# A row-wise log-sum-exp: the second pass as a section with its own semaphores, a shorter reduce in the check, and the first two loads issued as four transfers each, of every fourth partition

## The chip, the cores and the metric

The kernel runs on one core of one Trainium2 chip. The metric is the device time of that core in microseconds (us). All runs quoted here are at a granted clock of 1.000. A run's time is its profiled span plus 1.8 us, so differences in span can be compared with differences in time. Some words of this text: an *issue* is the instruction that starts a transfer; the DMA engines carry the transfer out in *packets*; it has *landed*, or is *complete*, with the last of its sixteen completions in the trace; an engine is *drained* when its own instructions are done and it goes to the final barrier.

## The reference

```python
batch, seq, dim = 32, 512, 1024
x = np.random.randn(batch, seq, dim).astype(np.float32)

max_x = np.max(x, axis=-1, keepdims=True)
return (max_x.squeeze(-1) + np.log(np.sum(np.exp(x - max_x), axis=-1))).astype(np.float32)
```

There are 16,384 rows of 1,024 values: 67.1 MB in, 64 KB out.

## The kernel before

Each of the 128 partitions holds 128 consecutive rows of `x`. The kernel skips the maximum: it takes `log(sum(exp(x)))` straight away, checks afterwards that no sum left a safe range, and only if one did does it run a second, stable pass. With this input it never does. The first two loads carry 16 rows per partition, which is one run of 64 KB in each partition.

```python
RING = 48
loads = [
    "R8 R8", "R8 R8", "R8 R8", "R7 R6 A A", "R6 R5 A A A", "R5 R4 A", "R5 R4", "R5 T3",
    "R3 A A A", "R3 A", "R2 T2", "R3", "R1 A", "T2", "T1", "A", "A",
]
ENGINES = [mybir.EngineType.SP, mybir.EngineType.Activation, mybir.EngineType.DVE]
...
def load(p0, c0, size):
    return nc.sync.dma_start(out=ring[:, p0 : p0 + size, :], in_=x_rows[:, c0 : c0 + size, :])
...
# per load: ScalarE exponentiates; VectorE adds up (R, T), or ScalarE does it itself (A)
...
nc.scalar.activation(out=res[:, EARLY:NC], in_=sumexp[:, EARLY:NC], func=AF.Ln)
nc.sync.dma_start(out=out_view, in_=res)

# the check: sums 0..126 within [1e-15, 1e15], the last row's maximum, the last sum
nc.vector.tensor_scalar(out=clamped[:, 0:LAST], in0=sumexp[:, 0:LAST], ...)
nc.vector.scalar_tensor_tensor(out=clamped[:, 0:LAST], ..., accum_out=bad[:, 0:1])
nc.tensor.matmul(count, lhsT=bad[:, 0:1], rhs=far, start=True, stop=False)
nc.vector.reduce_max(out=bad[:, 2:3], in_=last_row[:, 0, 0 : d // 4], axis=AX.X)
nc.vector.tensor_scalar(out=bad[:, 1:2], in0=bad[:, 2:3], ..., op0=ALU.is_lt)
nc.tensor.matmul(count, lhsT=bad[:, 1:2], rhs=far, start=False, stop=False)
nc.tensor.matmul(count, lhsT=sumexp[:, LAST:NC], rhs=ones, start=False, stop=True)
nc.vector.tensor_scalar(out=fine, in0=count, scalar1=HIGH, scalar2=None, op0=ALU.is_lt)
all_fine = nc.values_load(fine[0:1, 0:1], engines=ENGINES, ...)   # the flag, into registers
with tc.If(all_fine < 1, preferred_fallthrough_block=False):
    ...  # the second pass, with loads and store on SyncE: not taken with this input
```

`ENGINES` lists who reads the flag and branches: SyncE, ScalarE and VectorE. All five engines then meet at a final barrier (in the trace of before their last waits start at 163.99 to 164.04 us, and the span ends at 164.09).

Of the kernel before, what the change touches and what calls it, by code (L numbers as in the profile page):

```python
# [13 lines left out]
@with_exitstack  # L14
def kernel(
    ctx: ExitStack,
    tc: tile.TileContext,
    x: bass.AP,
    out: bass.AP,
):  # L20
    nc = tc.nc
    P = nc.NUM_PARTITIONS
    fp32 = mybir.dt.float32
    i32 = mybir.dt.int32
    AF = mybir.ActivationFunctionType
    AX = mybir.AxisListType
    ALU = mybir.AluOpType

    x_flat = x.flatten_outer_dims()
    n, d = x_flat.shape  # L30
    assert n % P == 0
    NC = n // P
    H = d // 2

    x_rows = x_flat.rearrange("(p c) d -> p c d", p=P)
    out_view = out.rearrange("a b -> (a b)").rearrange("(p c) -> p c", p=P)
# [8 lines that stand above are left out]
    ]  # L45
    loads = [[(op[0], int(op[1:] or 1)) for op in load.split()] for load in loads]
    assert sum(s for ops in loads for _, s in ops) == NC
    ENGINES = [mybir.EngineType.SP, mybir.EngineType.Activation, mybir.EngineType.DVE]
    EARLY = 104
    LAST = NC - 1  # L50

    big = ctx.enter_context(tc.tile_pool(name="big", bufs=1))
    stats = ctx.enter_context(tc.tile_pool(name="stats", bufs=1))
    psum = ctx.enter_context(tc.tile_pool(name="psum", bufs=1, space=bass.MemoryType.PSUM))

    ring = big.tile([P, RING, d], fp32, name="ring")
    sumexp = stats.tile([P, NC], fp32, name="sumexp")
    res = stats.tile([P, NC], fp32, name="res")
    clamped = stats.tile([P, NC], fp32, name="clamped")
    bad = stats.tile([P, 3], fp32, name="bad")  # L60
    fine = stats.tile([1, 1], i32, name="fine")
    far = stats.tile([P, 1], fp32, name="far")
    ones = stats.tile([P, 1], fp32, name="ones")
    last_exp = psum.tile([P, 1, d], fp32, name="last_exp")
    count = psum.tile([1, 1], fp32, name="count")

    nc.scalar.preload_act_table_set("natural_log_exp_and_others")  # L67
    nc.vector.memset(ones, 1.0)  # L68
    nc.vector.memset(far, 100 * HIGH)

    def load(p0, c0, size):
        return nc.sync.dma_start(out=ring[:, p0 : p0 + size, :], in_=x_rows[:, c0 : c0 + size, :])  # L72

    def without_wait(ins, group, reason):

        tc.declare_no_dep(ins.ins, group=group, reason=reason)

    c = 0
    p = 0
    for ops in loads:  # L80
        size = sum(s for _, s in ops)
        if p + size > RING:
            p = 0
        dma = load(p, c, size).ins
        for how, s in ops:
            v = ring[:, p : p + s, :]
            sums = sumexp[:, c : c + s]
            if how == "A":
                o = v if c < LAST else last_exp
                exp = nc.scalar.activation(out=o, in_=v, func=AF.Exp, accum_out=sums)  # L90
            else:
                exp = nc.scalar.activation(out=v, in_=v, func=AF.Exp)  # L92
            without_wait(exp, "loads", "the slot's earlier users came before this load")
            without_wait(exp, "exps", "the slot's earlier users came before this load")
            without_wait(exp, "sums", "the slot's earlier users came before this load")
            tc.add_to_no_dep_group("exps", exp.ins)
            added = []
            if how == "R":
                added = [nc.vector.reduce_sum(out=sums, in_=v, axis=AX.X)]  # L99
            elif how == "T":  # L100
                for r in range(s):
                    lo = ring[:, p + r, 0:H]
                    added.append(
                        nc.vector.scalar_tensor_tensor(  # L104
                            out=lo, in0=lo, scalar=1.0, in1=ring[:, p + r, H:d],
                            op0=ALU.mult, op1=ALU.add, accum_out=sums[:, r : r + 1],
                        )
                    )
            for add in added:
                tc.declare_no_dep(add.ins, dma, reason="ScalarE has waited for it")  # L110
                without_wait(add, "loads", "they came before this one")
            for add in added:
                tc.add_to_no_dep_group("sums", add.ins)
            c += s
            p += s
            last_row = v
        tc.add_to_no_dep_group("loads", dma)
        if c == EARLY + 14:
            nc.scalar.activation(out=res[:, 0:EARLY], in_=sumexp[:, 0:EARLY], func=AF.Ln)  # L119

    nc.scalar.activation(out=res[:, EARLY:NC], in_=sumexp[:, EARLY:NC], func=AF.Ln)  # L121
    nc.sync.dma_start(out=out_view, in_=res)




    nc.vector.tensor_scalar(  # L127
        out=clamped[:, 0:LAST], in0=sumexp[:, 0:LAST],
        scalar1=LOW, scalar2=HIGH, op0=ALU.max, op1=ALU.min,
    )  # L130
    nc.vector.scalar_tensor_tensor(  # L131
        out=clamped[:, 0:LAST], in0=clamped[:, 0:LAST], scalar=0.0, in1=sumexp[:, 0:LAST],
        op0=ALU.bypass, op1=ALU.not_equal, accum_out=bad[:, 0:1],
    )
    nc.tensor.matmul(count, lhsT=bad[:, 0:1], rhs=far, start=True, stop=False)  # L135
    nc.vector.reduce_max(out=bad[:, 2:3], in_=last_row[:, 0, 0 : d // 4], axis=AX.X)  # L136
    nc.vector.tensor_scalar(  # L137
        out=bad[:, 1:2], in0=bad[:, 2:3], scalar1=LOG_LOW, scalar2=None, op0=ALU.is_lt
    )
# [4 lines that stand above are left out]
    all_fine = nc.values_load(  # L144
        fine[0:1, 0:1], engines=ENGINES, min_val=0, max_val=1,
        skip_runtime_bounds_check_because="a truth value",
    )
    with tc.If(all_fine < 1, preferred_fallthrough_block=False):
        for c0 in range(0, NC, RING):
            s = min(RING, NC - c0)  # L150
            v = ring[:, 0:s, :]
            neg = clamped[:, c0 : c0 + s]
            load(0, c0, s)
            nc.vector.tensor_reduce(out=neg, in_=v, op=ALU.max, axis=AX.X, negate=True)
            nc.vector.tensor_add(out=v, in0=v, in1=neg[:, :, None].to_broadcast([P, s, d]))
            nc.scalar.activation(out=v, in_=v, func=AF.Exp)
            nc.vector.reduce_sum(out=sumexp[:, c0 : c0 + s], in_=v, axis=AX.X)
        nc.scalar.activation(out=res, in_=sumexp, func=AF.Ln)
        nc.vector.tensor_sub(out=res, in0=res, in1=clamped)
        nc.sync.dma_start(out=out_view, in_=res)  # L160


# [28 lines left out]
```

## Time and profile before

| | before |
|---|---|
| time | 165.29 us, median of 3 (165.22 to 165.62) |
| profiled span | 164.1 us, in a run of 165.87 us |
| DMA engines busy | 95.7% of the span |
| VectorE, ScalarE busy | 74%, 71% |
| first load packet starts (packet records of the trace) | 1.75 us |
| first load complete, by its sixteenth completion (trace) | 22.99 us |
| last load complete (trace) | 159.68 us |
| from there to the end of the span | 4.41 us |

The profiled run was slower than the median by 0.6 us.

These are lines of the page of the kernel before: its busy row, the DMA row in 40 slices, the DMA queue's line and the chain of waits.

```profile
PE 0.4 (0%) x6; PEld 0.2 (0%) x6; DVE 122.2 (74%) x44; ACT 116.8 (71%) x53; POOL 0.2 (0%) x4
...
DMA  7979998997997999899999989999999999999960
...
q1 hardware_dynamic: 2592, 67.18, 95.7%
...
DMA 64%; DVE 22%; ACT 11%; issue 1%; SPq 0%; PE 0%; DVEq 0%
```

The DMA engines are the bound: only the last two slices show them busy for less than 70%. The timeline of the kernel before, 0 to 24 us (start, length, engine, line, operation), shows the head: SyncE's first three load issues, merged in one line, and ScalarE's first work, which starts as the first load is complete.

```profile
0.73 1.33 SPq L72 DMA_DIRECT2D ring<-in_x_dram  x3
...
23.01 7.03 ACT L92 ACTIVATE ring<-ring 128x8192 f32<-128x8192 f32 x1 [21.00 <-DMA ring<-in_x_dram]
```

The windows view of the kernel before has the DMA share and GB/s as its last two columns. A packet's bytes and time are entered where it starts, so a share above 1 in a short window means that several packets began there. Loads begin between 1.7 and 2.0 us.

```profile
0.00:1.70 1.70, 0.00 (x0) 0.00 (x0) 0.09 (x2) 0.97 (x1) 0.20 (x4) 1.00 0.00 0
1.70:2.00 0.30, 0.00 (x0) 0.00 (x0) 0.00 (x0) 0.30 (x1) 0.00 (x0) 1.00 5.14 1748
```

The timeline of the kernel before from 160.3 us on shows the tail: two operations on 127 columns, the reduce, the compare, the output store's issue, and the flag.

```profile
160.19 0.23 DVE L127 TENSOR_SCALAR clamped<-sumexp 128x127 f32<-128x127 f32 x1
160.45 0.29 DVE L131 SCALAR_TENSOR_TENSOR clamped<-clamped,sumexp 128x127 f32<-128x127 f32 x1
...
160.66 0.41 DVE L136 TENSOR_REDUCE bad<-ring 128x1 f32<-128x256 f32 x1
...
161.11 0.15 DVE L137 TENSOR_SCALAR bad<-bad 128x1 f32<-128x1 f32 x1
161.15 0.35 SPq L122 DMA_DIRECT2D out_dram<-res  x1
...
161.60 0.14 DVE L143 TENSOR_SCALAR fine<-count 1x1 int32<-1x1 f32 x1 [0.33 <-PE count L141]
```

The view of the tile `fine` lists who reads the flag and for how long (minimum, median and maximum in ns).

```profile
L144 SPq TENSOR_LOAD <-fine x1: 462/462/462, 161.8 to 161.8; - x1
L144 ACTq TENSOR_LOAD <-fine x1: 469/469/469, 161.8 to 161.8; - x1
L144 DVEq TENSOR_LOAD <-fine x1: 543/543/543, 161.8 to 161.8; - x1
```

After the flag come instructions that the timeline leaves out (branches, semaphore waits). Their records say: VectorE was drained at 163.22 us, SyncE at 163.40, and the span ended 0.69 us after SyncE.

### The profile page before, as it was taken

Reading aid. Unit: us, or ns where it says so; the run is one execution under the profiler, and the core shown is the slowest. Engines: PE = TensorE matmul, PEld = TensorE weight load, DVE = VectorE, ACT = ScalarE, POOL = GpSimd, SP = SyncE. Lnnn points to the kernel's source line nnn. Section 1 sums busy time; section 2 is a strip of 40 time slices with the busy share of each in tenths; the row PEclk is TensorE's granted clock in tenths of the full one; section 3 lists DMA queues with packets and bytes.
Section 4 is the critical chain, followed back from the end, with each engine's and each line's share of the span. In section 5 each row is a group of like instructions: output and inputs, shape, how many; then the busy total and the mean of one; then the engine's idle time right before and its main releaser. Section 6 shows DMA issues by size and latency. Waiting matters only on the chain.

```text
span 164.1 us, 205 instructions
## 1 busy us (share of the span) xinstructions
PE 0.4 (0%) x6; PEld 0.2 (0%) x6; DVE 122.2 (74%) x44; ACT 116.8 (71%) x53; POOL 0.2 (0%) x4
## 2 busy tenths in 40 slices
PE   0000000000000000000000000000000000000001
PEld 0000000000000000000000000000000000000000
DVE  0000000699959999399999995999998999979893
ACT  3000039990699708995399929999969599999992
POOL 0000000000000000000000000000000000000000
DMA  7979998997997999899999989999999999999960
GB/s 256 511 335 431 511 399 367 511 463 304 511 431 335 511 450 404 374 464 479 433 447 419 433 365 449 419 432 440 417 439 415 433 425 419 415 421 423 409 248 20
DMA packets 2594, 67.19 MB, mean 409 GB/s; under 512 B 288, under 2 KB 416, under 8 KB 800
## 3 DMA queue, kind: packets, MB, share of 16 engines
q1 hardware_dynamic: 2592, 67.18, 95.7%
q14 instruction: 2, 0.02, 0.0%
HBM read 67.11 MB, written 0.07 MB: 409 GB/s over the span
## 4 chain that ended last, share of the span: by engine, by line
DMA 64%; DVE 22%; ACT 11%; issue 1%; SPq 0%; PE 0%; DVEq 0%
DMA ring<-in_x_dram 64%; DVE sumexp L99 20%; ACT ring L92 11%; DVE ring L104 1%; SPq L72 0%; DVE bad L136 0%; DVE clamped L127 0%; PE count L140 0%; DVE bad L137 0%; DVE clamped L131 0%; DVE fine L143 0%; PE count L141 0%; DVEq L127 0%
## 5 line engine op out<-in xcount | busy, mean ns | idle before, releaser
L99 DVE TENSOR_REDUCE sumexp<-ring 128x8 f32<-128x8192 f32 (+7 forms) x20 | 116.2, 5854 | 38.2 <-ACT ring L92 38.2
L92 ACT ACTIVATE ring<-ring 128x8192 f32<-128x8192 f32 (+7 forms) x24 | 101.7, 4283 | 43.6 <-DMA ring<-in_x_dram 43.6
L90 ACT ACTIVATE ring<-ring 128x1024 f32<-128x1024 f32 x12 | 12.5, 1039 | 0.0
L104 DVE SCALAR_TENSOR_TENSOR ring<-ring 128x512 f32<-128x512 f32 x8 | 5.1, 684 | 0.0
L90 ACT ACTIVATION_READ_ACCUMULATOR ring<-ring 128x1 f32 x12 | 2.2, 186 | 0.0
L67 ACT ACT_TABLE_LOAD x1 | 1.3, 1283 | 0.7 <-PEq L175 0.7
L90 ACT ACTIVATE last_exp<-ring 128x1024 f32<-128x1024 f32 x1 | 1.0, 1005 | 0.0
L68 DVE MEMSET ones<- 128x1 f32 x1 | 0.1, 59 | 0.8 <-PEq L175 0.8
L104 DVE DVE_READ_ACCUMULATOR ring<-ring 128x1 f32 x8 | 0.7, 82 | 0.0
L135 PE MATMUL count<-far,bad 128*1 128x1 f32 x2 | 0.2, 164 | 160.8 <-DVE clamped L131 160.8
L136 DVE TENSOR_REDUCE bad<-ring 128x1 f32<-128x256 f32 x1 | 0.4, 415 | 0.0
L143 DVE TENSOR_SCALAR fine<-count 1x1 int32<-1x1 f32 x1 | 0.1, 145 | 0.3 <-PE count L141 0.3
L131 DVE SCALAR_TENSOR_TENSOR clamped<-clamped,sumexp 128x127 f32<-128x127 f32 x1 | 0.3, 290 | 0.0
L127 DVE TENSOR_SCALAR clamped<-sumexp 128x127 f32<-128x127 f32 x1 | 0.2, 227 | 0.1
L135 PEld LDWEIGHTS count<-far,bad 128*1 128x1 f32 x2 | 0.1, 80 | 160.8 <-DVE clamped L131 160.8
L119 ACT ACTIVATE res<-sumexp 128x104 f32<-128x104 f32 x1 | 0.3, 273 | 0.0
L121 ACT ACTIVATE res<-sumexp 128x24 f32<-128x24 f32 x1 | 0.2, 222 | 0.0
L140 PE MATMUL count<-far,bad 128*1 128x1 f32 x2 | 0.2, 164 | 0.3 <-DVE bad L137 0.3
L141 PE MATMUL count<-ones,sumexp 128*1 128x1 f32 x2 | 0.2, 164 | 0.0
L90 ACT ACTIVATION_READ_ACCUMULATOR last_exp<-ring 128x1 f32 x1 | 0.2, 185 | 0.0
L137 DVE TENSOR_SCALAR bad<-bad 128x1 f32<-128x1 f32 x1 | 0.2, 154 | 0.0
L141 PEld LDWEIGHTS count<-ones,sumexp 128*1 128x1 f32 x2 | 0.1, 82 | 0.0
(7 smaller groups left out, 0.6 us busy)
## 6 DMA issues: line engine op xcount, KB each, us to landing
ring<-in_x_dram SPq DMA_DIRECT2D x1, 7680.0 KB, 33.1
ring<-in_x_dram SPq DMA_DIRECT2D x1, 7168.0 KB, 30.7
ring<-in_x_dram SPq DMA_DIRECT2D x1, 5120.0 KB, 31.4
ring<-in_x_dram SPq DMA_DIRECT2D x1, 4608.0 KB, 33.7
ring<-in_x_dram SPq DMA_DIRECT2D x1, 4096.0 KB, 29.4
ring<-in_x_dram SPq DMA_DIRECT2D x2, 2048.0 KB, 32.7
ring<-in_x_dram SPq DMA_DIRECT2D x1, 3072.0 KB, 36.3
ring<-in_x_dram SPq DMA_DIRECT2D x2, 1024.0 KB, 38.8
```

Of the source, the lines that this page charges most:

```text
L67: nc.scalar.preload_act_table_set("natural_log_exp_and_others")
L90: exp = nc.scalar.activation(out=o, in_=v, func=AF.Exp, accum_out=sums)
L92: exp = nc.scalar.activation(out=v, in_=v, func=AF.Exp)
L99: added = [nc.vector.reduce_sum(out=sums, in_=v, axis=AX.X)]
L104: nc.vector.scalar_tensor_tensor(out=lo, in0=lo, scalar=1.0, in1=ring[:, p + r, H:d], op0=ALU.mult, op1=ALU.add, accum_out=sums[:, r : r + 1],
L119: nc.scalar.activation(out=res[:, 0:EARLY], in_=sumexp[:, 0:EARLY], func=AF.Ln)
L121: nc.scalar.activation(out=res[:, EARLY:NC], in_=sumexp[:, EARLY:NC], func=AF.Ln)
L127: nc.vector.tensor_scalar(out=clamped[:, 0:LAST], in0=sumexp[:, 0:LAST], scalar1=LOW, scalar2=HIGH, op0=ALU.max, op1=ALU.min,)
L131: nc.vector.scalar_tensor_tensor(out=clamped[:, 0:LAST], in0=clamped[:, 0:LAST], scalar=0.0, in1=sumexp[:, 0:LAST], op0=ALU.bypass, op1=AL ...
L135: nc.tensor.matmul(count, lhsT=bad[:, 0:1], rhs=far, start=True, stop=False)
L136: nc.vector.reduce_max(out=bad[:, 2:3], in_=last_row[:, 0, 0 : d // 4], axis=AX.X)
L141: nc.tensor.matmul(count, lhsT=sumexp[:, LAST:NC], rhs=ones, start=False, stop=True)
```

## The change

The second pass becomes a section with two semaphores of its own, all its transfers issued from ScalarE, so SyncE no longer reads the flag. The reduce in the check goes over 64 columns instead of 256. And each of the first two loads is issued as four transfers, of every fourth partition, so that each hands the DMA engines a quarter of the rows at a time.

```diff
-    ENGINES = [mybir.EngineType.SP, mybir.EngineType.Activation, mybir.EngineType.DVE]
+    ENGINES = [mybir.EngineType.Activation, mybir.EngineType.DVE]
...
     def load(p0, c0, size):
-        return nc.sync.dma_start(out=ring[:, p0 : p0 + size, :], in_=x_rows[:, c0 : c0 + size, :])
+        step = 4 if c0 < 2 * 16 else 1
+        return [
+            nc.sync.dma_start(
+                out=ring[k::step, p0 : p0 + size, :], in_=x_rows[k::step, c0 : c0 + size, :]
+            ).ins
+            for k in range(step)
+        ]
...
-    nc.vector.reduce_max(out=bad[:, 2:3], in_=last_row[:, 0, 0 : d // 4], axis=AX.X)
+    nc.vector.reduce_max(out=bad[:, 2:3], in_=last_row[:, 0, 0 : d // 16], axis=AX.X)
...
     with tc.If(all_fine < 1, preferred_fallthrough_block=False):
-        for c0 in range(0, NC, RING):
-            ...
-            load(0, c0, s)
-            ...
+        with tc.tile_critical(sync_engine=mybir.EngineType.Activation):
+            with nc.semaphore("landed") as landed, nc.semaphore("ready") as ready:
+                for c0 in range(0, NC, RING):
+                    ...
+                    nc.scalar.dma_start(out=v, in_=x_rows[:, c0 : c0 + s, :]).then_inc(landed, 16)
+                    ...
```

More of the change, by code (lines that the diff above doesn't have):

```diff
@@ L83 @@
             p = 0
-        dma = load(p, c, size).ins
+        dmas = load(p, c, size)
         for how, s in ops:
@@ L109 @@
             for add in added:
-                tc.declare_no_dep(add.ins, dma, reason="ScalarE has waited for it")
+                for dma in dmas:
+                    tc.declare_no_dep(add.ins, dma, reason="ScalarE has waited for it")
                 without_wait(add, "loads", "they came before this one")
@@ L116 @@
             last_row = v
-        tc.add_to_no_dep_group("loads", dma)
+        for dma in dmas:
+            tc.add_to_no_dep_group("loads", dma)
         if c == EARLY + 14:
@@ L148 @@
     with tc.If(all_fine < 1, preferred_fallthrough_block=False):
-        for c0 in range(0, NC, RING):
-            s = min(RING, NC - c0)
-            v = ring[:, 0:s, :]
-            neg = clamped[:, c0 : c0 + s]
-            load(0, c0, s)
-            nc.vector.tensor_reduce(out=neg, in_=v, op=ALU.max, axis=AX.X, negate=True)
-            nc.vector.tensor_add(out=v, in0=v, in1=neg[:, :, None].to_broadcast([P, s, d]))
-            nc.scalar.activation(out=v, in_=v, func=AF.Exp)
-            nc.vector.reduce_sum(out=sumexp[:, c0 : c0 + s], in_=v, axis=AX.X)
@@ L158 @@
-        nc.scalar.activation(out=res, in_=sumexp, func=AF.Ln)
-        nc.vector.tensor_sub(out=res, in0=res, in1=clamped)
-        nc.sync.dma_start(out=out_view, in_=res)
+        with tc.tile_critical(sync_engine=mybir.EngineType.Activation):
+            with nc.semaphore("landed") as landed, nc.semaphore("ready") as ready:
+                rows = 0
+                steps = 0
+                for c0 in range(0, NC, RING):
+                    s = min(RING, NC - c0)
+                    v = ring[:, 0:s, :]
+                    neg = clamped[:, c0 : c0 + s]
+                    if c0:
+                        nc.scalar.wait_ge(ready, steps)
+                    nc.scalar.dma_start(out=v, in_=x_rows[:, c0 : c0 + s, :]).then_inc(landed, 16)
+                    rows += 16
+                    nc.vector.wait_ge(landed, rows)
+                    nc.vector.tensor_reduce(
+                        out=neg, in_=v, op=ALU.max, axis=AX.X, negate=True
+                    ).then_inc(ready, 1)
+                    nc.vector.wait_ge(ready, steps + 1)
+                    nc.vector.tensor_add(
+                        out=v, in0=v, in1=neg[:, :, None].to_broadcast([P, s, d])
+                    ).then_inc(ready, 1)
+                    nc.scalar.wait_ge(ready, steps + 2)
+                    nc.scalar.activation(out=v, in_=v, func=AF.Exp).then_inc(ready, 1)
+                    nc.vector.wait_ge(ready, steps + 3)
+                    nc.vector.reduce_sum(
+                        out=sumexp[:, c0 : c0 + s], in_=v, axis=AX.X
+                    ).then_inc(ready, 1)
+                    steps += 4
+                nc.scalar.wait_ge(ready, steps)
+                nc.scalar.activation(out=res, in_=sumexp, func=AF.Ln).then_inc(ready, 1)
+                nc.vector.wait_ge(ready, steps + 1)
+                nc.vector.tensor_sub(out=res, in0=res, in1=clamped).then_inc(ready, 1)
+                nc.scalar.wait_ge(ready, steps + 2)
+                nc.scalar.dma_start(out=out_view, in_=res).then_inc(landed, 16)
+                nc.scalar.wait_ge(landed, rows + 16)
```

## The prediction

> **What bounds the kernel now.** The loads. The page counts 67.1 MB over the 164.1 us span (409 GB/s), the 16 DMA engines busy 95.7%; VectorE 74%, ScalarE 71%. In the chain of waits, loads of `ring` hold 64%. The trace's packets show first load packets from 1.75 us and the last load landing at 159.7 us; in between no DMA engine lacks work: each later load is issued about 30 us before it lands. A 64 KB packet takes 2.42 us, 27 GB/s; sixteen of those are 433 GB/s. The change moves the same bytes, so it can gain only at the ends: the head, and a tail of 4.4 us from the last landing to the span's end.
>
> **Head.** Today one issue queues 128 rows, eight 64 KB rows per DMA engine. The sixteen first packets start staggered, from 1.75 to 2.83 us, and the first load's completions spread from 22.20 to 22.99 us: an engine that starts late stays late. A first issue of 32 rows is two rows per engine; if the stagger is the time to hand out descriptors, it should shrink to about a quarter, 0.3 us. [...] Eight issues at 0.43 us (trace) take SyncE 3.4 us, but two rows per engine last 4.9 us, so nothing starves. The ninth transfer waits for the first quarter, about 7 us, with 14 MB still queued. Expected: first load complete 0.5 to 0.8 us sooner, last load 0.2 to 0.6 us. Later stages move along.
>
> **Tail.** SyncE today: output store issued 161.15, flag read 161.77 (0.46 us), branch, four semaphore updates, branch at 162.70, seven waits, drained at 163.40. VectorE drained at 163.23, ScalarE at 162.97; the store landed at 162.70. Without the flag read SyncE drains by about 162.9. VectorE then ends the kernel: 0.17 us gained. The reduce over 64 instead of 256 columns (0.415 us now, about 1 ns per column) takes 0.2 us from the chain reduce, compare, matmul, flag, read, branch; ScalarE's `sumexp`, ready at 160.87, does not take over. One more semaphore wait before that reduce should hide. Sum: 0.3 to 0.4 us.
>
> **Not on the path.** The second pass's section is not executed with this input; its waits stand inside the branch not taken. The final barrier remains.
>
> **Time.** 165.29 - 0.4 - 0.35, rounded up: 164.6 us, range 163.9 to 165.6. Faster by over 2% 0.03, within 2% 0.88, slower 0.09.
>
> **What would show it.** Right: first packets of all engines start within about 0.4 us; first load complete at about 22.3 us; SyncE drained before VectorE; last landing to end of span about 4.0 us. Wrong: first packets far over 2.42 us, fewer than 16 engines, or gaps in the DMA busy row in the first 40 us.
>
> **What would make it wrong.** [...] Or the stagger is no descriptor cost and stays: about 165.0.

The sum has all its terms: 165.29 - 0.4 - 0.35 = 164.54, put at 164.6. That 32 rows are two for each engine was an assumption.

## The result

The changed kernel takes 165.41 us (median of 6, 165.26 to 165.84) against 165.31 (median of 6, 165.22 to 165.62). The ratio is 1.0004, with a 95% interval of 0.9990 to 1.0019: the same. A ratio here is the mean time of one kernel's runs over that of the other's of the same rounds, so not quite the ratio of the medians that are quoted. The prediction had named a clear gain of 0.7 us, and there is none.

The page of the changed kernel, the same lines:

```profile
PE 0.4 (0%) x6; PEld 0.2 (0%) x6; DVE 122.0 (75%) x44; ACT 116.7 (71%) x53; POOL 0.2 (0%) x4
...
DMA  7979979979988998999999999999999999999970
...
q1 hardware_dynamic: 2688, 67.18, 95.9%
...
DMA 61%; DVE 22%; ACT 12%; SPq 3%; issue 1%; PE 0%; DVEq 0%; ACTq 0%
```

The 3% of SPq in the chain is new: the loads' issues now stand in it. The timeline of the changed kernel at the head (nine load issues merged, the ninth of them after a wait: by the records it starts at 8.91 us, and the first quarter is complete at 8.89):

```profile
0.73 8.53 SPq L75 DMA_DIRECT2D ring<-in_x_dram  x9
...
23.55 7.03 ACT L99 ACTIVATE ring<-ring 128x8192 f32<-128x8192 f32 x1 [21.54 <-DMA ring<-in_x_dram]
```

ScalarE's first work starts at 23.55 us instead of 23.01: later, where the prediction had it earlier. The windows of the changed kernel show where that begins. No load packet starts before 2.0 us:

```profile
1.70:2.00 0.30, 0.00 (x0) 0.00 (x0) 0.00 (x0) 0.30 (x1) 0.00 (x0) 1.00 0.00 0
2.00:3.00 1.00, 0.00 (x0) 0.00 (x0) 0.00 (x0) 0.01 (x1) 0.00 (x0) 1.00 2.40 786
```

The issue records show half of the delay: the first issue takes 0.54 us, not 0.38, and the seven after it 0.57 to 0.73, not 0.43. The other half comes after the issue: the first packet starts 0.79 us after the end of the first issue, not 0.64, so at 2.05 us, not 1.75. The sixteen first packets spread from 2.05 to 3.33 us, 1.28 us where it was 1.08: the stagger did not shrink. The first load is complete at 23.45 us, against 22.99.

The tail of the changed kernel, on the other hand, did what was intended. Its timeline from 160.2 us on:

```profile
160.23 0.29 DVE L140 SCALAR_TENSOR_TENSOR clamped<-clamped,sumexp 128x127 f32<-128x127 f32 x1
...
160.45 0.21 DVE L145 TENSOR_REDUCE bad<-ring 128x1 f32<-128x64 f32 x1
...
160.70 0.15 DVE L146 TENSOR_SCALAR bad<-bad 128x1 f32<-128x1 f32 x1
...
160.96 0.35 SPq L131 DMA_DIRECT2D out_dram<-res  x1
161.18 0.15 DVE L152 TENSOR_SCALAR fine<-count 1x1 int32<-1x1 f32 x1 [0.33 <-PE count L150]
```

And the readers of `fine` in the changed kernel:

```profile
L153 ACTq TENSOR_LOAD <-fine x1: 465/465/465, 161.4 to 161.4; - x1
L153 DVEq TENSOR_LOAD <-fine x1: 672/672/672, 161.4 to 161.4; - x1
```

The reduce is 0.2 us shorter, SyncE reads no flag, and the last landing (159.50 us) is 4.13 us from the end of the span instead of 4.41. VectorE's flag read, though, grew from 0.543 to 0.672 us.

One thing does not add up yet. By these two profiles the first load is 0.46 us late in the changed kernel, but the last load is 0.18 us early. The packet records show that in the profile of before seven 64 KB packets that began between 41.2 and 42.0 us took 2.79 to 3.04 us instead of 2.42; the completions of one load, spread over 0.8 us until then, spread over 1.3 us from the third load on. Either that was a stray event in one run, or it belongs to the kernel before and the split cures it. So the theory to test is: the split costs about 0.4 us at the head, the tail saves about 0.3, and the two cancel. The rivals: the split is neutral and the tail's saving never reaches the time; or the split helps by a steadier rate.

### The profile page after: what moved, and what is told of

Its sections match the earlier page's. It is cut to its first block, busy times and chain, and to the rows that moved or that the text cites. A ratio compares the mean times of both kernels' runs of the same rounds, so it can differ in the third digit from the quotient of the medians.

```text
span 163.6 us, 211 instructions
## 1 busy us (share of the span) xinstructions
PE 0.4 (0%) x6; PEld 0.2 (0%) x6; DVE 122.0 (75%) x44; ACT 116.7 (71%) x53; POOL 0.2 (0%) x4
## 4 chain that ended last, share of the span: by engine, by line
DMA 61%; DVE 22%; ACT 12%; SPq 3%; issue 1%; PE 0%; DVEq 0%; ACTq 0%
DMA ring<-in_x_dram 61%; DVE sumexp L106 20%; ACT ring L99 12%; SPq L75 3%; DVE ring L111 1%; DVE clamped L136 0%; PE count L149 0%; DVE bad L146 0%; DVE clamped L140 0%; DVE fine L152 0%; DVE bad L145 0%; PE count L150 0%; DVEq L145 0%; ACTq L99 0%; DVEq L136 0%
```

## The experiments

All kernels gave correct results. The table sums them up; first packet, first load and tail are from the one profiled run of each kernel.

| run | what it is | median us | ratio (95%) | first packet | first load complete | last landing to end |
|---|---|---|---|---|---|---|
| e1 | before again | 165.29 | 0.9999 (0.9986 to 1.0013) | 1.74 | 22.86 | 4.38 |
| e2 | before + split | 165.82 | 1.0027 (1.0013 to 1.0040) | 2.06 | 23.44 | 4.40 |
| e3 | changed, no split | 165.16 | 0.9983 (0.9969 to 0.9996) | 1.73 | 23.17 | 4.12 |
| e4 | before + short reduce | 165.19 | 0.9989 (0.9975 to 1.0003) | 1.73 | 23.01 | 4.23 |
| e5 | before + split of second load only | 165.32 | 0.9995 (0.9982 to 1.0008) | 1.74 | 23.04 | 4.41 |
| e6 | before + split in neighbouring rows | 207.26 | 1.2531 (1.2513 to 1.2550) | 1.74 | 43.92 | 4.39 |
| e7 | before + split in columns | 166.33 | 1.0062 (1.0042 to 1.0083) | 1.74 | 22.99 | 4.38 |
| e8 | before + split in two | 165.87 | 1.0034 (1.0021 to 1.0047) | 2.05 | 23.32 | 4.40 |
| e9 | before + section | 165.27 | 0.9988 (0.9975 to 1.0001) | 1.75 | 22.95 | 4.22 |
| e10 | e3 again | 165.14 | 0.9984 (0.9971 to 0.9997) | 1.74 | 23.09 | 4.14 |
| e11 | changed again | 165.46 | 1.0006 (0.9993 to 1.0019) | 2.06 | 23.40 | 4.13 |
| e12 | e3 + early check | 165.13 | 0.9983 (0.9964 to 1.0003) | 1.74 | 23.03 | 4.07 |

### e1: the kernel before, once more

No edit.

> The kernel before, unchanged, a second profile. In the first profile of it seven 64 KB packets that started between 41.2 and 42.0 us took 2.8 to 3.0 us instead of 2.42, and the completions of one load spread over 1.3 us from then on, against 0.8 before; that run was 165.87 us where the median is 165.31. Theory (that was a stray event of one run, and the two profiles at hand may not be compared landing by landing after 41 us): here no such packets, completions of the third load within 0.9 us, last load landed at 159.1 to 159.3 us, span 163.5. Rival (it belongs to the kernel before, and the split removes it): the slow packets at 41 us are here again, span 164.1, last landing 159.7. Time 165.3 in both, ratio 1.000.

Measured: 165.29 us, ratio 0.9999. In its profile (a run of 165.10 us) there are no such packets, the third load's completions lie within 0.74 us, the last load is complete at 158.94 us and the span is 163.3. So the slow packets do not belong to every run of the kernel before. But they were no single event either: e9 has eight packets of 2.9 to 3.3 us at 36 to 37 us and eight of 2.8 to 3.1 at 41 to 42, e10 six of 2.6 to 2.8 at 41 to 42, and e2 five of 2.7 to 2.9 at 51 to 52. In e3 and e12 packets are slow by less, 35 and 14 of them over 2.5 us (none in e1, e4 and e5 after the first microseconds). The last landing moves with such packets: with an unsplit first load it is at 158.94 to 159.18 us in e1, e4, e5 and e10, but at 159.52 to 159.71 in e3, e9, e12 and before; with the strided one it is at 159.43 to 159.64 in all four profiles. The two ranges overlap, so single profiles cannot settle what the split costs; the medians of the runs below do. Whether a split of the second load prevents slow packets at 41 to 42 us is not shown: three of the seven profiles with that load in one piece have them, none of the six with it in strided rows or in columns.

### e2, e3 and e4: the parts one by one

e2 takes the new `load` (and the lists of transfers that go with it) into the kernel before. e3 takes it out of the changed kernel. e4 has only the reduce.

```diff
 e3, against the changed kernel
-        step = 4 if c0 < 2 * 16 else 1
+        step = 1
 e4, against the kernel before
-    nc.vector.reduce_max(out=bad[:, 2:3], in_=last_row[:, 0, 0 : d // 4], axis=AX.X)
+    nc.vector.reduce_max(out=bad[:, 2:3], in_=last_row[:, 0, 0 : d // 16], axis=AX.X)
```

> Only the first two loads as four transfers each of every fourth row; tail as before. Theory (the split costs at the head what the tail saves): issues of 0.54 to 0.6 us instead of 0.38 to 0.43, first packet at 2.05 instead of 1.75, stagger 1.1 to 1.3 us, first load complete at 23.4 instead of 23.0; time 165.31 + 0.4 = 165.7, ratio 1.0025. Rival A (the split is neutral and the tail's saving is not seen in the time): 165.3, ratio 1.000. Rival B (the split helps by the steadier rate after 41 us): 165.1 or less.

> The changed kernel with the first two loads each as one transfer again: section for the second pass, SyncE out of the branch, reduce over 64 columns. Theory: 165.31 - 0.35 to 0.4 = 164.95, ratio 0.998; from last landing to end of span 4.1 us or less (4.41 in the first profile of before); first packet at 1.75. Rival A (the tail's saving is not seen in the time): 165.3, ratio 1.000. Rival B: 165.3 to 165.5.

> Only the reduce over 64 instead of 256 columns, its 0.415 us down to 0.214. It lies on the chain reduce, compare, matmul, flag, read, branch of every engine that branches, so by the theory all of it shows: 165.1, ratio 0.9988, and the flag is written 0.2 us sooner after the last landing. Rival A: 165.3.

The split alone is slower, by 0.27% or 0.45 us (0.0027 of 165.3), and its interval excludes 1. Its stagger was 0.89 us, less than the 1.1 to 1.3 expected and less than the 1.08 of before, and still its first load was complete at 23.44 us: the loss does not come from the stagger. The rest alone is faster, by 0.17% or 0.28 us, and its interval excludes 1 as well. The sum, +0.17 us, lies within the interval of the changed kernel's own ratio (-0.17 to +0.31 us). So both rivals fall: the change is a loss and a gain that nearly cancel. The head of e2, from its timeline, is the changed kernel's head:

```profile
0.73 8.52 SPq L75 DMA_DIRECT2D ring<-in_x_dram  x9
...
23.55 7.03 ACT L99 ACTIVATE ring<-ring 128x8192 f32<-128x8192 f32 x1 [21.53 <-DMA ring<-in_x_dram]
```

e3 gains less than the 0.35 to 0.4 us expected, 0.28. e4's interval just includes 1; its tail is 4.23 us in the profile, 0.15 less than e1's.

### e5: the split without the first load

```diff
 against e2
-        step = 4 if c0 < 2 * 16 else 1
+        step = 4 if c0 == 16 else 1
```

> Only the second load as four transfers of every fourth row; the first load is one transfer, tail as before. Theory (the split costs only through the first issue, which all DMA engines wait for): first packet at 1.75 us as before, first load complete at 22.9 to 23.1, second not later than 42.4, time 165.3, ratio 1.000. Rival (each transfer of 32 rows costs the engines something, whichever load it is): half or more of the 0.5 us of the split of both loads, 165.5 to 165.8, and the second load's completion late by itself.

165.32 us, ratio 0.9995. The four strided issues are long here too (0.52 to 0.91 us, and 0.62 for the plain one right after them), the second load arrives in the same four quarters, and nothing is lost: its completion is at 42.38 us, as in before (42.34). The timeline of e5:

```profile
0.73 3.86 SPq L75 DMA_DIRECT2D ring<-in_x_dram  x6
...
23.07 7.03 ACT L99 ACTIVATE ring<-ring 128x8192 f32<-128x8192 f32 x1 [21.05 <-DMA ring<-in_x_dram]
```

So it is the first load's split that costs. Here, with the 8 MB of the first load queued before them, the long issues hid (ratio 0.9995). This run also disposes of the stagger: its first packets were spread over 1.56 us (1.74 to 3.30), the widest of the unsplit ones, and the first load was complete at 23.04 us all the same. A late start is in part made up within the first packet: in e5 the four packets that start last (3.06 to 3.30 us) take 2.42 to 2.43 us, the five that start first (1.74 to 2.02) 3.07 to 3.32. The sixteen first packets end on average at 5.16 to 5.27 us in the eight profiles with the first load in one piece, whatever the stagger, and at 5.54 to 5.62 us in the four with a strided one. So the loss of about 0.4 us is complete when the first packets end.

### e6: quarters of neighbouring rows

```diff
 against e2
-                out=ring[k::step, p0 : p0 + size, :], in_=x_rows[k::step, c0 : c0 + size, :]
+                out=ring[k * 128 // step : (k + 1) * 128 // step, p0 : p0 + size, :],
+                in_=x_rows[k * 128 // step : (k + 1) * 128 // step, c0 : c0 + size, :],
```

> The split with 32 neighbouring rows in each transfer instead of every fourth row. For the issue: if the stride makes the issue long (0.54 instead of 0.38 us) and the start late, here the issue is 0.38 to 0.43 and the first packet at 1.75; if the row count does it, 0.54 and 2.05 as with the stride. [...]a 64 KB packet should take about 4.8 us instead of 2.42 and the first two loads about 19 us longer each, 203 us; rival: packets of 2.42 us and 165.3 to 165.8[...].

This tells two things. The first issue takes 0.38 us and the first packet starts at 1.74 us, as without a split. So the long issue and the late start come with the stride, not with the row count or the number of transfers. The windows of e6 and then of e8 (below, stride of two) for the same 0.3 us show it:

```profile
1.70:2.00 0.30, 0.00 (x0) 0.00 (x0) 0.00 (x0) 0.30 (x1) 0.00 (x0) 1.00 11.66 2621
...
1.70:2.00 0.30, 0.00 (x0) 0.00 (x0) 0.00 (x0) 0.30 (x1) 0.00 (x0) 1.00 0.00 0
```

And the time is 207 us, where 203 was expected. These are the DMA rows of e6's page (40 slices of 5.1 us) and two stretches from its windows view:

```profile
DMA  9999999999999999999998899989999999999990
GB/s 204 204 204 204 204 204 204 204 204 204 204 204 204 204 217 204 396 408 434 514 443 383 383 515 391 480 362 470 423 431 402 437 440 408 421 418 430 415 381 18
```

```profile
2.00:43.00 41.00, 0.00 (x0) 0.00 (x0) 0.00 (x0) 0.01 (x1) 0.00 (x0) 1.00 1.01 209
...
84.00:125.00 41.00, 0.00 (x0) 0.00 (x0) 31.50 (x4) 31.04 (x5) 0.00 (x0) 1.00 0.99 428
```

While the quarters of neighbouring rows arrive, the engines are as busy as ever at half the rate: a 64 KB packet takes about 5.1 us instead of 2.42, and sixteen of them for each engine account for the 42 us lost (16 x 2.6). Over those stretches the trace has 204 to 209 GB/s; why the packets are slow is not shown. The stride of four in the change is not an ornament, though: with it nearly every packet after each engine's first takes 2.42 us. Of the splits by rows that were tried, only those with a stride kept that pace, and they pay for it at the first issue.

### e7 and e8: other ways to split

```diff
 e7, against e2
-                out=ring[k::step, p0 : p0 + size, :], in_=x_rows[k::step, c0 : c0 + size, :]
+                out=ring[:, p0 + k * size // step : p0 + (k + 1) * size // step, :],
+                in_=x_rows[:, c0 + k * size // step : c0 + (k + 1) * size // step, :],
 e8, against e2
-        step = 4 if c0 < 2 * 16 else 1
+        step = 2 if c0 < 2 * 16 else 1
```

> The first two loads as four transfers of all 128 partitions and a quarter of the columns (16 KB packets, eight per engine and transfer). Theory (the long issue and late start belong to the 32-row pattern): issues of 0.38 to 0.43 us, first packet at 1.75, stagger of the first packets still 0.9 to 1.1 us as it does not depend on the bytes or rows handed out, packets of 0.614 us (427 GB/s as measured for 16 KB later in the kernel, against 434), which costs 1.6 percent of 39 us or 0.6 us if the rate of the packets is what ends the load: 165.9, ratio 1.004. Rival (any four issues instead of one start late): first packet at 2.05.

> The first two loads as two transfers each, of every second row (64 rows, four per engine). If the issue's length goes with the stride being more than one: issue 0.54, first packet 2.05, time 165.7 to 165.8 as with four. If it goes with the row count or with the four: in between, issue 0.45, first packet 1.9, 165.5. [...]

e8: issue 0.55 us, first packet 2.05, 165.87 us. A stride of two costs what a stride of four costs (e2: first packet 2.06, 165.82 us); it is having a stride, not the size of it or the count of transfers. Packets stay at 2.42 us. e7: the head is as the theory has it (issue 0.38, first packet 1.74, first load complete at 22.99 us, as in before). But the time is worse than the 165.9 us expected and uneven, 165.63 to 167.14 us over six runs where the kernel before spread over 0.4. The profiled run was the quickest of the six, so what the slow ones lose is not in a profile. That stays open.

### e9 to e12: the tail

e9 has only the section (the changed kernel with `step = 1` and `d // 4`), e10 is e3 again, and e11 is the changed kernel again, on the same chip. e12 builds on e3: it makes the range check of the first 104 sums in mid-kernel, where VectorE waits anyway (it is busy for 74% of the span in before), and leaves 23 columns for the end.

```diff
 e12, against e3 (in_range holds the two VectorE operations and the matmul)
+            in_range(0, EARLY, 0)          # after the load that completes 118 columns
...
-    (the two operations on columns 0 to 126 and their matmul)
+    in_range(EARLY, LAST, 3)
```

> Only the section with own semaphores, with SyncE out of the branch; reduce over 256 columns and unsplit loads as before. Theory: SyncE drained no longer after VectorE by 0.17 to 0.22 us as before, VectorE's drain ends the kernel, last landing to end of span 4.2 to 4.3 us (before 4.38 to 4.41), time 165.2, ratio 0.999; together with the reduce (0.9989) it gives the 0.9983 of both. Rival (the section costs the branch something, such as a longer way to jump): 165.3 or more.

> The changed kernel without the split once more, as its first interval reached 0.9996: ratio 0.997 to 0.999 again, time 165.0 to 165.2.

> The changed kernel on the same chip as the one without the split. Theory (the two parts add): slower than that one by 0.4 to 0.5 us, at 165.4 to 165.6, ratio to before 1.000 to 1.001.

> The changed kernel without the split, and the range check of the first 104 sums made while VectorE waits in mid-kernel, so that the two operations on 127 columns after the last sum become two on 23 (0.227 and 0.29 us, about 1 ns a column: 0.2 us off VectorE's chain). ScalarE's last sum is ready 0.16 us before VectorE's chain gets to the matmul, so at most 0.16 us shows: 164.9 to 165.0, ratio 0.9975. Rival (the flag read on VectorE grew from 0.54 to 0.67 us where the flag came 0.2 us sooner; it ends a fixed time after the output store's issue, whenever it starts): no gain over the kernel without the split, 165.1.

e10 repeats e3 (0.9984, after 0.9983), and e11 repeats the changed kernel (1.0006, after 1.0004), 0.3 us slower in the median than e10 on the same chip; 0.4 to 0.5 was expected, and the intervals allow both. The section alone is worth 0.12% (0.2 us), with an interval that just reaches 1. The tail's account, in us after the last landing, from the instruction records of one profile each:

| | e1 before | e4 reduce | e9 section | e10 both | changed | e12 early check |
|---|---|---|---|---|---|---|
| flag written | 2.02 | 1.83 | 2.04 | 1.83 | 1.82 | 1.68 |
| VectorE's flag read takes | 0.546 | 0.666 | 0.546 | 0.674 | 0.672 | 0.542 |
| VectorE drained | 3.50 | 3.43 | 3.51 | 3.44 | 3.43 | 3.15 |
| SyncE drained | 3.68 | 3.54 | 3.37 | 3.37 | 3.15 | 3.38 |
| span ends | 4.38 | 4.23 | 4.22 | 4.14 | 4.13 | 4.07 |

The span ends 0.7 us after the later of the two, in every column. In before that is SyncE, by 0.18 us. With the section it is VectorE, at 3.51, so the gain stops there. The reduce brings the flag 0.19 us forward, but VectorE's read of it then takes 0.13 us longer, so VectorE is through only 0.07 us sooner. e12 shows that this is no rule that the read must end a fixed time after the store's issue: with the flag 0.15 us sooner still, the read is back at 0.542. Why it lengthens at just that moment stays open.

In its median time e12 (165.13 us, 164.9 to 165.0 expected) looks like the rival, with no gain over e3, but its six runs lie apart (three at 164.84 to 164.94 us, three at 165.32 to 165.88), so the time does not settle it. The profile shows a gain in the tail of 0.07 us over e10, and what limits it, which is not the rival's reason. Its VectorE is through at 3.15 us, 0.29 sooner than in e10, but now SyncE is last, at 3.38. Its waits in the trace explain it, here from the view of who waited for whom on SyncE's queue in e12:

```profile
SPq L221 <- DMA out_dram<-res: 1.1, 1, 1.1
```

In e3, e9, e10 and e12 the output store's semaphore is waited for early among SyncE's final waits. The store lands 3.0 us after the last load (3.02 in before, 3.00 in the changed kernel), and several further waits follow it, some 0.06 us apart. In the changed kernel, where the order of the semaphores is another (the split adds six transfers; that this turns the order was not tested by itself), the store's wait happens to come last, and SyncE is drained at 3.15. An order with the early check and the store waited for last was not run; from these columns it could end near 3.15 + 0.7 = 3.85 us, an estimate.

The version that beats both kernels is the changed one without the split (e3 and e10: 165.16 and 165.14 us, both intervals below 1). The gain is 0.26 to 0.28 us, far below 2%.

## Why the prediction was wrong

- **What bounds the kernel: right.** The loads do, and only head and tail could give anything. e5 and e6 confirm it from both sides: long issues behind a full queue cost nothing (165.32 us), and a slower packet costs its full length (42 us in e6).
- **Head: wrong in sign.** The step that failed is "if the stagger is the time to hand out descriptors, it should shrink to about a quarter, 0.3 us"; what the stagger is, no run shows. With two strided rows per engine the stagger was 0.89 to 1.36 us (changed, e2, e11), with four (e8) 1.50, with eight 0.96 to 1.56 (before, e1, e3, e4, e5, e9, e10, e12); only the neighbouring rows of e6 had less, 0.64, at packets of 5.1 us. Nor does it decide the end of the load, as e2 and e5 showed: "an engine that starts late stays late" was the second weak link. Expected was a first load complete 0.5 to 0.8 us sooner; it is about 0.4 us later (23.32 to 23.45 us in the four strided profiles, 22.86 to 23.17 in the eight with one piece).
- **The term that was left out of the sum.** "Eight issues at 0.43 us (trace)" took the length of an unstrided issue for a strided one. A strided issue takes 0.54 to 0.6 us and more. The seven later ones hide, as predicted ("nothing starves"), but the first stands in front of all the engines: its packet starts 0.31 us late, 0.16 through the longer issue and 0.15 between the issue's end and the packet. From first packet to complete load it then takes 21.3 to 21.4 us in the four profiles with a strided first load, and 21.1 to 21.4 in the nine with an unsplit or column-split one, so the late start is most of the loss; the rest, about 0.1 us, has no cause shown, and is within the scatter of the profiles. The prediction's own way out, that the stagger "stays: about 165.0", had the stagger right and missed this cost.
- **Sixteen engines for 32 rows: right, though only assumed.** In the changed kernel each quarter had sixteen completions, and the quarters of the first load were complete at 8.89, 13.72, 18.60 and 23.45 us: 4.83 to 4.88 us apart, two packets of 2.42. Packets "far over 2.42 us", which would have shown the prediction wrong, did not come with the stride beyond each engine's first, and came without it (e6, 5.1 us a packet).
- **Tail: right in mechanism, somewhat too large.** Predicted 0.3 to 0.4 us, measured 0.26 to 0.28 in the time. SyncE did drain before VectorE, and the reduce did save 0.2 us on the chain. There was some luck in the first: "drains by about 162.9" (3.2 us after the last landing) came true in the changed kernel (3.15), where the store's wait is last; without the split it is 3.37, only 0.07 before VectorE (e10). The mis-sized term is the reduce's 0.2 us, of which VectorE's longer flag read (0.67 instead of 0.54 us) gave 0.13 back.
- **Not on the path: right.** The section's own semaphores and waits stand in the branch that is not taken; e9, which has all of them, loses nothing.
- **Sum.** -0.4 - 0.35 became +0.45 - 0.28, and 164.6 us became 165.41.

## What to carry to other kernels

In this kernel, bound by its loads, the first issue is the one whose length could not hide (0.54 us with a stride, 0.38 without), so try the plainest pattern there and put clever patterns behind a full queue (e5: nothing lost). Of the splits by rows, those with a stride of two or four kept the packet at 2.42 us and those of neighbouring rows did not (5.1), and the stride had its price at the issue. When two small parts of one change point in opposite directions, run each alone, with five rounds, and take a second profile of the kernel before: a stray 0.6 us in a single profile was as large as everything that was to be explained.

## Further figures that the traces gave

- Length of an issue by its pattern, without a stride: 0.38 us for the first, mostly 0.41 to 0.49 for those right behind another (once 0.66 and once 0.81), 0.33 to 0.35 for later ones that stand alone. With every second or fourth row: 0.54 to 0.55 for the first, 0.52 to 0.91 for those behind it; first packet 0.31 us later. Whether the stride on the memory side or on the HBM side does it was not separated.
- From the end of the first issue to the first packet: 0.62 to 0.64 us without a stride, 0.78 to 0.80 with one; from the issue's start 1.00 to 1.02 and 1.33 us. The sixteen first packets then start over 0.9 to 1.6 us (0.64 in e6), and those that start first take up to 3.6 us.
- Which engine takes which partitions is not shown. For 32 strided rows the runs show only that packets keep 2.42 us, and for 32 neighbouring rows 5.1 us and 204 to 209 GB/s.
- `tensor_load`, the instruction that reads the flag here: ScalarE and SyncE took 0.46 to 0.49 us in all profiles but one (0.53), and VectorE 0.54 to 0.67.
- Stray slow packets: seven of 2.8 to 3.0 us instead of 2.42 in one profile of before, none in the next, sixteen of 2.8 to 3.3 in e9; their cause is not shown. The runs of the kernel before spread over 0.4 us (165.22 to 165.62).
